# Low parts of split weights on another engine, and one unit further ahead

## The chip, the cores and the metric

The kernel runs on one core of one Trainium2 chip. The metric is the time of one launch in device microseconds, median of three runs. The engines' names in the rows are PE (TensorE matmuls), PEld (TensorE weight loads), DVE (VectorE), ACT (ScalarE), POOL (GpSimd) and SP (SyncE, which issues most loads).

## The reference

256 tokens of 1024 features pass through three blocks of float32 layers, one after the other:

```
x = first_block(x):    # two layers
    layer 0: mix = [ssd_mixer(x @ w_in), short_conv(x @ w_in)] @ w_out     # Mamba-2 with a gated convolution
    layer 1: mix = sliding_window_attention(x @ w_qkv) @ w_o               # 16 heads of 64, window 128
    both:    x = layer_norm(alpha * x + mix)
             x = layer_norm(alpha * x + (silu(x @ w_gate) * (x @ w_up)) @ w_down)
             x = x + (p @ w_ple) * sigmoid(x @ w_ple_gate + b)
x = second_block(x, c):
    h = rms_norm(x) * (1 + scale) + shift;  z = h @ w_in
    x = x + gate * ([rwkv7(z), stick_breaking_attention(z)] @ w_out)
    x = x + gate2 * moe(rms_norm(x) * ...)                                  # 32 experts, top 4, 403 MB
x = third_block(x, c):
    proj = (rms_norm(x) * (1 + scale) + shift) @ w_in                       # 14 column groups
    y_mla = attention(rms(q_lat) @ w_uq, rms(kv_lat) @ w_ukv);  y_mb = moba(q, k, v)
    y = (g_a * (y_mla @ w_o_mla) + g_b * (y_mb @ w_o_moba)) @ w_out
    x = x + gate * rms_norm(y)
```

## The kernel before, in words

Activations lie feature-major, [128, 8, 256]. The blocks run in sequence: the SSD layer, its feed-forward part with the gated embedding (ple), the attention layer, its feed-forward part, the mixer of the second block, its experts, and the third block. Outside the experts every dense product works with split weights. A float32 weight tile w becomes a high part hi, rounded to the F32R format by a copy on ScalarE (tile `wh`, L309), and a low part lo = w - hi (tile `wl`, L310). The activations are split in the same way, and a product is three matmuls, hi·xh, hi·xl and lo·xh (helper `mm`, L511).

Weights arrive in a ring of eight 1 MB tiles, loaded on SyncE's queue in the order of a plan that is written ahead (class `Stream`). A unit is 128 x 1024 weights: one `wh`, one `wl`, and 24 matmuls of TensorE. `unit(name, n)` (L333) gives the next unit to its user, and splits units ahead until n are split that have not been used up (`ahead`, L317). So each call puts a copy into ScalarE's queue and a subtraction into that of GpSimd or VectorE at that place of the program. The pool of split parts has three buffers of each part. A load is issued when the last unit of an older tile has been split.

The low part goes to GpSimd for each third unit (u % 3 == 0), else to `self.rest`. That is VectorE, but GpSimd in the attention layer from the first head to the end of w_o (L1021 to L1029), and in the whole third block (L2229). The engines take their instructions in the order of the program, which is written by hand (a manual schedule); no planner moves anything. What VectorE has besides low parts are evictions of sums from PSUM, splits of activations, norms (a square root is a chain of small operations, `rsqrt1` at L530 to L545 with tiles q1..., `rsqrt` at L515 to L525 with tiles r4...), and the row maxima of the attentions.

The attentions (`attention`, L1034) run a head or two at a time between units of a dense product ("ticks"): a head's scores, the row maximum (L1049), its scaling (L1052), the exponent on ScalarE, the division of the probabilities (L1083), transposes, and the product with the values. The latent norm of the third block (L2300 to L2309) is such a background chain too. `rows_norm` (L654) takes the last two units of a layer's last product and computes the layer norm behind them.

Of the kernel before, what the change touches and what calls it, by code (L numbers as in the profile page):

```python
# [22 lines left out]
F32 = mybir.dt.float32  # L23
# [227 lines left out]
class Stream:  # L251


    def __init__(self, kb, plan, ring=8):
        self.kb, self.ring = kb, ring
        self.plan = []
        self.units = []
        self.fence = []
        unit = 1024
        for e in plan:  # L260
            if e == "end":
                self.fence.append(len(self.units))
                continue
            i = len(self.plan)
            self.plan.append(e)
            name, r0, nk, c0, n, split = e
            h = nk if not split else max(1, unit // n)
            for k in range(0, nk, h):
                self.units.append((i, k, min(h, nk - k), k + h >= nk, split))
        self.raws = {}  # L270
        self.splits = {}
        self.nsplit = self.used = 0
        self.pending = None
        self.rest = kb.nc.vector
        self.room, self.nload = ring, 0

    def _retire(self, i):
        self.room += 1
        self.load()
# [19 lines left out]
    def _split(self, u):  # L299
        kb = self.kb  # L300
        i, k0, nk, last, split = self.units[u]
        if not split:
            return
        n = self.plan[i][4]
        self.load()
        w = self.raws[i][:, k0:k0 + nk, :]
        hi = kb.tl(kb.hpool, [128, nk, n], F32R, "wh")
        lo = kb.tl(kb.hpool, [128, nk, n], F32R, "wl")
        kb.nc.scalar.activation(hi, w, AF.Copy)  # L309
        (kb.nc.gpsimd if u % 3 == 0 else self.rest).tensor_sub(lo, w, hi.bitcast(F32))  # L310
        self.splits[u] = (hi, lo)
        if last:
            self._retire(i)
# [16 lines left out]
        self.ahead(n)  # L330
        return u

    def unit(self, name, n=2):  # L333

        return self.splits.pop(self._next(name, n))

    def raw(self, name, n=2):

# [47 lines left out]
class KB:  # L386
# [196 lines left out]
    def dense_F(self, name, x, nk=8, n=512, tag="acc", tail=False, ready=None, ticks=1):  # L583


        ps = [self.tl(self.pp, [128, 2, T], F32, tag) for _ in range((n + 255) // 256)]
        k = 0
        held = []
        while k < nk:
            if ready:  # L590
                ready(k)
            step = max(1, 1024 // n)
            last = k + step >= nk
            if tail and k + 2 * step >= nk and not last:
                held.append((k, self.st.unit(name)))
                k += step
                continue
            held.append((k, self.st.unit(name, 1 if held else 2)))
            for b in range(len(ps)):
                for k0, (hi, lo) in held:  # L600
                    for kk in range(hi.shape[1]):
                        for c in range(2 * b, min(2 * b + 2, (n + 127) // 128)):
                            s = slice(c * 128, min(n, c * 128 + 128))
                            self.mm3(ps[b][0:s.stop - s.start, c % 2], (hi[:, kk, s], lo[:, kk, s]),
                                     (x[0][:, k0 + kk], x[1][:, k0 + kk]), start=(k0 + kk == 0 and c % 2 == 0))
            k += step
            held = []
            for _ in range(ticks):
                self.tick()
        return ps  # L610
# [43 lines left out]
    def rows_norm(self, name, x, nk, ps, nm, i, fill, parts=None, ready=None):  # L654


        nc, P = self.nc, self.xpool
        self.rows_T(name, x, 0, nk - 2, ps, ready)
        if ready:
            ready(nk - 1)  # L660
        us = [(nk - 2, self.st.unit(name)), (nk - 1, self.st.unit(name, 1))]
        xn = self.tl(P, [128, 2, 1024], F32, "xn")
        half = [slice(0, 512), slice(512, 1024)]
        for t in range(2):
# [29 lines left out]
        xf = self.tl(self.fpool, [128, 8, T], F32, "xf")  # L694
# [273 lines left out]
    def att_layer(self, xf, x):  # L968
        nc = self.nc
# [5 lines left out]
        for u in range(4):  # L975
            hi, lo = self.st.unit("w_qkv")
            for kk in range(2):
                k = u * 2 + kk
# [35 lines left out]
        for h in range(2):  # L1014
            ps = self.dense_F("w_qkv", x, ticks=1 + h)
            for j in range(4):
                c = 4 * h + j
                nc.vector.tensor_scalar(qT[:, c], ps[j // 2][:, j % 2], self.col("b_qk", c), 0.125, op0=OP.add, op1=OP.mult)
            if h == 0:
                self.bg = self.attention(P, [head(i) for i in range(16)], self.band, 1.0)  # L1020
                self.st.rest = nc.gpsimd  # L1021
        ps = self.residual(xa, self.ident)

        def ready(k):
# [1 line left out]
                self.tick()  # L1026

        r = self.rows_norm("w_o", ox, 8, ps, "lnm", 1, self.cond_fill(1), ready=ready)
        self.st.rest = nc.vector  # L1029
        es.close()  # L1030
        return r

# [258 lines left out]
    def mixer(self, xf, stat):  # L1291
        nc, pp, st = self.nc, self.pp, self.st
        es = ExitStack()
        X = self.xpool
# [3 lines left out]
        vs = self.tl(P, [128, 2, 512], F32, "m")  # L1298
        hes = ExitStack()
        self.hpool = hes.enter_context(self.pool("wsplit2", 3))  # L1300
        self.st.fence.pop(0)
        t4 = lambda tag: self.tl(P, [128, 4, T], F32, tag)
        c4 = lambda ap: ap.rearrange("p j (t s) -> p j t s", s=128)
        S = math.exp(-0.5)
        x = (self.tl(X, [128, 8, T], F32R, "xh"), self.tl(X, [128, 8, T], F32R, "xl"))
# [169 lines left out]
        hes = ExitStack()  # L1475
# [15 lines left out]
        hes = ExitStack()  # L1491
# [731 lines left out]
    def third(self, xf, stat, P):  # L2223
        nc, pp = self.nc, self.pp
        es = ExitStack()
        X = self.xpool
        hes = ExitStack()
        self.hpool = hes.enter_context(self.pool("wsplit4", 3))
        self.st.rest = nc.gpsimd  # L2229
        t4 = lambda tag, dt=F32: self.tl(P, [128, 4, T], dt, tag)  # L2230
        x = (self.tl(X, [128, 8, T], F32R, "xh"), self.tl(X, [128, 8, T], F32R, "xl"))
        self.ada_norm(xf, X, self.col("g_pre", 0, 8), self.mod3[:, 8:16], self.mod3[:, 0:8], x, stat, 3, 8)
        dense = lambda **kw: self.dense_F("w_in_3", x, **kw)
        two = lambda ap: ap[:, 0:1].to_broadcast([128, 2, T])
        ag = self.tl(P, [128, 8], F32, "ag")
# [180 lines left out]
        for i in (1, 0):  # L2416
            g[i] = self.tl(X if i == 0 else P, [128, 8, T], F32, "xn" if i == 0 else "gb")
            for h in range(2):
                ps = dense()
                for j in range(4):  # L2420
                    k = 4 * h + j
                    nc.scalar.activation(g[i][:, k], ps[j // 2][:, j % 2], AF.Tanh, bias=hb[:, 8 * i + k:8 * i + k + 1], scale=0.5)

        for i, name in ((1, "moba"), (0, "mla")):
# [3 lines left out]
            if i == 0:  # L2428
                x = (self.tl(X, [128, 8, T], F32R, "xh"), self.tl(X, [128, 8, T], F32R, "xl"))
# [42 lines left out]
    def run(self):  # L2472
        nc, tc = self.nc, self.tc
        with ExitStack() as es:
# [4 lines left out]
            self.wpool = es.enter_context(self.pool("w", 8))  # L2479
            self.xpool = es.enter_context(self.pool("x", 1))  # L2480
            hes = ExitStack()
            self.hpool = hes.enter_context(self.pool("wsplit", 3))
            self.pp = outer.enter_context(tc.tile_pool(name="ps", bufs=2, space=PSUM))
            outer.enter_context(tc.manual_schedule())
            _tl = self.tl
# [8 lines left out]
            xf = self.tl(self.fpool, [128, 8, T], F32, "xf")  # L2494
# [11 lines left out]
            if "ssd" in self.stages:  # L2506
                xf, x, ready = self.ssd_layer(xf)
                xf, x = self.ffn_ple(0, xf, x, ready)
                self.dbg("xc0", xf)
            else:  # L2510
                stat = None
                x = self.resplit(xf, self.xpool)
            if "att" in self.stages:
                xf, x, ready = self.att_layer(xf, x)
                xf, stat = self.ffn_ple(1, xf, x, ready)
# [45 lines left out]
```

## Time and profile before

| | |
|---|---|
| median of three runs | 2303.5 us (2303.3 to 2306.31) |
| the profiled execution | 2300.47 us, its span 2298.7 us |
| mean granted clock of TensorE | 0.973 |
| TensorE busy | 2140.1 us (93%) |
| VectorE busy | 1038.7 us (45%) |
| ScalarE busy | 725.5 us (32%) |
| GpSimd busy | 452.9 us (20%) |
| DMA | 618.06 MB, of them 403 MB experts |

The layers run to 806 us, the mixer from there to 1080, the experts to 2026, the third block to the end. The rows below come from five views. Windows give for each stretch (start and end in us, then its length) the busy time of each engine in us with its instructions in brackets, then the granted clock of TensorE as a share of full speed, the share of the DMA engines that is busy, and GB/s. Waits give the engine, operation and line that waited, the releaser, and the us in total, the times and the longest. The view of a line gives the operation, count, shortest, median and longest in ns. The timeline gives start and duration in us, engine, line, operation, output and inputs. Groups of instructions give busy us and mean ns of one, then the idle time before them.

### The profile page before, as it was taken

The numbers are of one execution on the slowest core, as the hardware profiler recorded it, in microseconds if no ns is written. First come the engines' busy times: TensorE is split into PE (matmuls) and PEld (weight loads), VectorE is DVE, ScalarE is ACT, GpSimd is POOL, SyncE is SP. The second block draws the span as 40 slices with busy tenths as digits, with TensorE's granted clock in tenths as the row PEclk, the third lists the DMA queues.
The fourth block names the chain that finished last, engine by engine and source line by source line (L and its number), as shares of the span: only waits on it lengthen the run. The fifth ranks groups of instructions, "written<-read, shape, count | busy, mean of one in ns | idle before, by whom it ended". The sixth has DMA issues, their size and how long they took to land.

```text
span 2298.7 us, 31686 instructions
## 1 busy us (share of the span) xinstructions
PE 2140.1 (93%) x13242; PEld 1505.3 (65%) x13242; DVE 1038.7 (45%) x1937; ACT 725.5 (32%) x1169; POOL 452.9 (20%) x220
## 2 busy tenths in 40 slices
PE   7999999989999987888899999999999999989997
PEld 7897998887898877778444444344443333377886
DVE  6674676556677658756222222322222211144653
ACT  5444543545543553333111110111111011033552
POOL 2322232223232234221000000000000000056453
PEclk9999999999999999989899999999999999999998
DMA  7434767432767632105799999999999999963320
GB/s 297 157 130 146 274 262 272 177 129 74 282 261 284 233 127 83 65 1 204 317 426 427 427 423 427 427 428 427 428 428 427 428 427 427 426 242 132 114 70 19
DMA packets 62100, 618.06 MB, mean 269 GB/s; under 512 B 7648, under 2 KB 10720, under 8 KB 12672
## 3 DMA queue, kind: packets, MB, share of 16 engines
q1 hardware_dynamic: 58768, 612.33, 66.3%
q10 hardware_dynamic: 3184, 3.65, 0.5%
q8 instruction: 106, 1.74, 0.3%
q14 instruction: 42, 0.34, 0.0%
HBM read 614.90 MB, written 1.05 MB: 268 GB/s over the span
## 4 chain that ended last, share of the span: by engine, by line
PE 34%; DMA 12%; DVE 4%; ACT 1%; issue 0%; POOL 0%; ACTq 0%; DVEq 0%; SPq 0%; POOLq 0%
PE acc L511 21%; DMA expert<-exp_w 12%; PE py L511 10%; PE tp L511 2%; DVE an L1052 1%; PE tp L2036 0%; DVE pr L1083 0%; ACT pr L1075 0%; PE tp L2028 0%; DVE am L1049 0%; DVE q1t L543 0%; POOL wl L310 0%; DVE kf L2357 0%; DVE qf L2465 0%; DVE ot L2399 0%
## 5 line engine op out<-in xcount | busy, mean ns | idle before, releaser
L511 PE MATMUL acc<-xh,wh 128*128 128x256 f32 (+1 forms) x1736 | 496.0, 289 | 16.1 <-ACT wh L309 13.0
L511 PE MATMUL acc<-xh,wl 128*128 128x256 f32 (+2 forms) x1704 | 485.8, 285 | 18.3 <-POOL wl L310 9.4
L511 PE MATMUL acc<-xl,wh 128*128 128x256 f32 (+1 forms) x1736 | 487.9, 285 | 1.4 <-DVE xl L1284 1.3
L511 PE MATMUL acc<-expert,xe 128*64 128x512 f32 x2048 | 457.0, 597 | 18.0 <-DMA expert<-exp_w 15.7
L511 PEld LDWEIGHTS acc<-xh,wh 128*128 128x128 f32 (+1 forms) x1736 | 330.0, 191 | 24.7 <-ACT wh L309 13.6
L511 PEld LDWEIGHTS acc<-expert,xe 128*64 128x64 f32 x2048 | 144.8, 137 | 299.4 <-issue 282.0
L511 PEld LDWEIGHTS acc<-xh,wl 128*128 128x128 f32 (+2 forms) x1704 | 326.0, 191 | 22.6 <-POOL wl L310 11.5
L511 PEld LDWEIGHTS acc<-xl,wh 128*128 128x128 f32 (+1 forms) x1736 | 329.8, 191 | 4.8 <-DVE xl L1284 1.9
L310 POOL TENSOR_TENSOR wl<-w_w_in,wh 128x1024 fp32r<-128x1024 f32 (+1 forms) x49 | 119.0, 2435 | 1079.0 <-ACT wh L309 1068.5
L511 PE MATMUL py<-expert,aT 128*64 128x512 f32 x1024 | 235.3, 602 | 4.0 <-DMA expert<-exp_w 3.3
L2011 ACT ACTIVATE s<-a 128x512 f32<-128x512 f32 x32 | 20.2, 630 | 529.9 <-DVE a L2010 529.8
L2071 DVE SCALAR_TENSOR_TENSOR xf<-py,mod,xf 128x256 f32<-128x256 f32 x128 | 55.6, 479 | 279.8 <-PE py L511 279.8
L2010 DVE TENSOR_SCALAR a<-acc 128x512 f32<-128x512 f32 x32 | 22.1, 692 | 346.3 <-PE acc L511 346.3
L511 PEld LDWEIGHTS py<-expert,aT 128*64 128x64 f32 x1024 | 72.1, 138 | 138.2 <-issue 128.8
L1224 DVE SCALAR_TENSOR_TENSOR w_ada_t<-w_ada_t,pe 128x1024 f32<-128x1024 f32 x56 | 93.2, 1687 | 0.0
L309 ACT ACTIVATE wh<-w_w_in 128x1024 fp32r<-128x1024 f32 (+1 forms) x66 | 68.4, 1046 | 38.0 <-PE acc L511 32.0
L2058 ACT ACTIVATE y<-py 64x512 f32<-64x512 f32 x64 | 37.9, 592 | 117.5 <-PE py L511 116.9
L511 PE MATMUL tp<-sel,xh 128*128 128x128 f32 x512 | 63.5, 285 | 7.9 <-ACT aT L2038 6.9
L309 ACT ACTIVATE wh<-w_w_ffn_down 128x1024 fp32r<-128x1024 f32 x44 | 46.8, 1064 | 69.3 <-PE acc L511 69.3
L511 PE MATMUL acc<-wh,hh 128*128 128x512 f32 x176 | 68.7, 390 | 0.0
L511 PE MATMUL acc<-wh,hl 128*128 128x512 f32 x176 | 68.5, 389 | 0.0
L511 PE MATMUL acc<-wl,hh 128*128 128x512 f32 x176 | 68.5, 389 | 0.0
(659 smaller groups left out, 3405.0 us busy)
## 6 DMA issues: line engine op xcount, KB each, us to landing
expert<-exp_w SPq DMA_DIRECT2D x191, 2048.0 KB, 28.9
w_w_in<-tiles SPq DMA_DIRECT2D x31, 1024.0 KB, 4.8
w_ada_t<-tiles SPq DMA_DIRECT2D x28, 1024.0 KB, 6.9
w_w_ffn_gate<-tiles SPq DMA_DIRECT2D x22, 1024.0 KB, 4.8
w_w_ffn_up<-tiles SPq DMA_DIRECT2D x22, 1024.0 KB, 5.6
w_w_ffn_down<-tiles SPq DMA_DIRECT2D x22, 1024.0 KB, 5.6
w_w_in_mix<-tiles SPq DMA_DIRECT2D x21, 1024.0 KB, 7.4
w_w_out_mix<-tiles SPq DMA_DIRECT2D x8, 1024.0 KB, 4.8
```

The costliest lines, as they stand in the source:

```text
L309: kb.nc.scalar.activation(hi, w, AF.Copy)
L310: (kb.nc.gpsimd if u % 3 == 0 else self.rest).tensor_sub(lo, w, hi.bitcast(F32))
L511: self.nc.tensor.matmul(out, lhsT, rhs, start=start, stop=True, skip_group_check=True)
L1052: nc.vector.tensor_scalar(nm, m, -scale, None, op0=OP.mult)
L1224: self.nc.vector.scalar_tensor_tensor(w[:, j], w[:, j], 1.0, crow[:, int(m >= 48)], op0=OP.mult, op1=OP.mult, accum_out=dst)
L2010: nc.vector.tensor_scalar(a, pg, 7.0, None, op0=OP.min)
L2011: nc.scalar.activation(s, a, AF.Sigmoid, scale=1.702)
L2058: nc.scalar.activation(y[r, o], py[r], AF.Copy)
L2071: nc.vector.scalar_tensor_tensor(xf[:, k], ps[o][:, c], gate2(k), xf[:, k], op0=OP.mult, op1=OP.add)
```

## The change

Three things change. `Stream._split` picks the engine of a low part by a rule: GpSimd only for each third unit of `w_in_mix`, `w_out_mix`, `w_out_3`, of `w_in_3` but for one column group, and of the feed-forward weights but for their first piece; VectorE for all others, those of the attention layer's w_qkv and w_o, of the ple gates, of the mixer and of two thirds of the third block among them. `unit` splits three units ahead where it split two (`self.depth`), in the layers and in the third block; the mixer sets it back to two. The pools of split parts have four buffers of each part in the layers and in the third block. The stretches of raw weights keep their two.

```
@@ -271,8 +271,8 @@
         self.splits = {}
         self.nsplit = self.used = 0
         self.pending = None
-        self.rest = kb.nc.vector
         self.room, self.nload = ring, 0
+        self.depth = 3
 
     def _retire(self, i):
         self.room += 1
@@ -307,7 +307,10 @@
         hi = kb.tl(kb.hpool, [128, nk, n], F32R, "wh")
         lo = kb.tl(kb.hpool, [128, nk, n], F32R, "wl")
         kb.nc.scalar.activation(hi, w, AF.Copy)
-        (kb.nc.gpsimd if u % 3 == 0 else self.rest).tensor_sub(lo, w, hi.bitcast(F32))
+        name, r0, _, c0, _, _ = self.plan[i]
+
+        far = u % 3 == 0 and (name in ("w_in_mix", "w_out_mix", "w_out_3") or name == "w_in_3" and c0 != 928 or name[:5] == "w_ffn" and r0 + c0)
+        (kb.nc.gpsimd if far else kb.nc.vector).tensor_sub(lo, w, hi.bitcast(F32))
         self.splits[u] = (hi, lo)
         if last:
             self._retire(i)
@@ -330,9 +333,9 @@
         self.ahead(n)
         return u
 
-    def unit(self, name, n=2):
-
-        return self.splits.pop(self._next(name, n))
+    def unit(self, name, n=None):
+
+        return self.splits.pop(self._next(name, n or self.depth))
 
     def raw(self, name, n=2):
 
@@ -595,7 +598,7 @@
                 held.append((k, self.st.unit(name)))
                 k += step
                 continue
-            held.append((k, self.st.unit(name, 1 if held else 2)))
+            held.append((k, self.st.unit(name, self.st.depth - len(held))))
             for b in range(len(ps)):
                 for k0, (hi, lo) in held:
                     for kk in range(hi.shape[1]):
@@ -658,7 +661,7 @@
         self.rows_T(name, x, 0, nk - 2, ps, ready)
         if ready:
             ready(nk - 1)
-        us = [(nk - 2, self.st.unit(name)), (nk - 1, self.st.unit(name, 1))]
+        us = [(nk - 2, self.st.unit(name)), (nk - 1, self.st.unit(name, self.st.depth - 1))]
         xn = self.tl(P, [128, 2, 1024], F32, "xn")
         half = [slice(0, 512), slice(512, 1024)]
         for t in range(2):
@@ -1018,7 +1021,6 @@
                 nc.vector.tensor_scalar(qT[:, c], ps[j // 2][:, j % 2], self.col("b_qk", c), 0.125, op0=OP.add, op1=OP.mult)
             if h == 0:
                 self.bg = self.attention(P, [head(i) for i in range(16)], self.band, 1.0)
-                self.st.rest = nc.gpsimd
         ps = self.residual(xa, self.ident)
 
         def ready(k):
@@ -1026,7 +1028,6 @@
                 self.tick()
 
         r = self.rows_norm("w_o", ox, 8, ps, "lnm", 1, self.cond_fill(1), ready=ready)
-        self.st.rest = nc.vector
         es.close()
         return r
 
@@ -1298,6 +1299,7 @@
         vs = self.tl(P, [128, 2, 512], F32, "m")
         hes = ExitStack()
         self.hpool = hes.enter_context(self.pool("wsplit2", 3))
+        self.st.depth = 2
         self.st.fence.pop(0)
         t4 = lambda tag: self.tl(P, [128, 4, T], F32, tag)
         c4 = lambda ap: ap.rearrange("p j (t s) -> p j t s", s=128)
@@ -2225,11 +2227,10 @@
         es = ExitStack()
         X = self.xpool
         hes = ExitStack()
-        self.hpool = hes.enter_context(self.pool("wsplit4", 3))
-        self.st.rest = nc.gpsimd
+        self.hpool = hes.enter_context(self.pool("wsplit4", 4))
         t4 = lambda tag, dt=F32: self.tl(P, [128, 4, T], dt, tag)
         x = (self.tl(X, [128, 8, T], F32R, "xh"), self.tl(X, [128, 8, T], F32R, "xl"))
-        self.ada_norm(xf, X, self.col("g_pre", 0, 8), self.mod3[:, 8:16], self.mod3[:, 0:8], x, stat, 3, 8)
+        self.ada_norm(xf, X, self.col("g_pre", 0, 8), self.mod3[:, 8:16], self.mod3[:, 0:8], x, stat, 2, 8)
         dense = lambda **kw: self.dense_F("w_in_3", x, **kw)
         two = lambda ap: ap[:, 0:1].to_broadcast([128, 2, T])
         ag = self.tl(P, [128, 8], F32, "ag")
@@ -2479,7 +2480,7 @@
             self.wpool = es.enter_context(self.pool("w", 8))
             self.xpool = es.enter_context(self.pool("x", 1))
             hes = ExitStack()
-            self.hpool = hes.enter_context(self.pool("wsplit", 3))
+            self.hpool = hes.enter_context(self.pool("wsplit", 4))
             self.pp = outer.enter_context(tc.tile_pool(name="ps", bufs=2, space=PSUM))
             outer.enter_context(tc.manual_schedule())
             _tl = self.tl
```

Line numbers move by up to three: L310 is L313 in the new kernel, L545 is L548, L1049 is L1050. By the order of both kernels, 79 low parts leave GpSimd for VectorE; TensorE and SyncE have the same instructions in the same order.

The first place is the end of the SSD layer on VectorE: the last low parts in front of the layer norm (`bst` are its statistics). Before:

```order
L310 TENSOR_TENSOR wl_2144<-w_w_out_mix_1670,wh_2143 128x1024
L310 TENSOR_TENSOR wl_2178<-w_w_out_mix_1728,wh_2177 128x1024
L310 TENSOR_TENSOR wl_2196<-w_w_out_mix_1804,wh_2195 128x1024
L310 TENSOR_TENSOR wl_2230<-w_w_ffn_gate_36_2113,wh_2229 128x1024
L675 BN_STATS bst_2290<-acc_1894 128x6
L675 BN_STATS bst_2290<-acc_1895 128x6
L676 BN_AGGR bmv_2291<-bst_2290 128x2
L535 TENSOR_SCALAR q1v_269_2296<-bmv_2291 128x1
L538 TENSOR_SCALAR q1y_272_2299<-q1v_269_2296 128x1
```

After:

```order
L313 TENSOR_TENSOR wl_2132<-w_w_out_mix_1646,wh_2131 128x1024
L313 TENSOR_TENSOR wl_2166<-w_w_out_mix_1704,wh_2165 128x1024
L313 TENSOR_TENSOR wl_2184<-w_w_out_mix_1780,wh_2183 128x1024
L313 TENSOR_TENSOR wl_2218<-w_w_ffn_gate_36_2101,wh_2217 128x1024
L313 TENSOR_TENSOR wl_2234<-w_w_ffn_gate_36_2101,wh_2233 128x1024
L678 BN_STATS bst_2290<-acc_1898 128x6
L678 BN_STATS bst_2290<-acc_1899 128x6
L679 BN_AGGR bmv_2291<-bst_2290 128x2
L538 TENSOR_SCALAR q1v_269_2296<-bmv_2291 128x1
L541 TENSOR_SCALAR q1y_272_2299<-q1v_269_2296 128x1
```

One more low part of the first feed-forward piece stands in VectorE's queue ahead of the norm; before, the one that was split last there was GpSimd's.

The second place is the start of the third block, on VectorE: the first norm (q1v, q1y, q1h, q1t are its square root). Before:

```order
L2071 SCALAR_TENSOR_TENSOR xf_7643<-py_14413,mod_14_122,xf_7643 128x256 x2
L2071 SCALAR_TENSOR_TENSOR xf_7643<-py_14414,mod_14_122,xf_7643 128x256 x2
L1265 SCALAR_TENSOR_TENSOR ada_14475<-mod_15_123,cols_95 128x8
L537 TENSOR_SCALAR q1v_1852_14491<-tp_14425 128x2
L538 TENSOR_SCALAR q1y_1855_14494<-q1v_1852_14491 128x2
L539 TENSOR_SCALAR q1h_1853_14492<-q1v_1852_14491 128x2
```

and GpSimd, at the same place:

```order
L310 TENSOR_TENSOR wl_14478<-w_w_in_0_14454,wh_14477 128x1024
L310 TENSOR_TENSOR wl_14482<-w_w_in_0_14454,wh_14481 128x1024
L310 TENSOR_TENSOR wl_14488<-w_w_in_1_14456,wh_14487 128x1024
L310 TENSOR_TENSOR wl_14578<-w_w_in_1_14456,wh_14577 128x1024
L310 TENSOR_TENSOR wl_14608<-w_w_in_2_14458,wh_14607 128x1024
L310 TENSOR_TENSOR wl_14636<-w_w_in_2_14458,wh_14635 128x1024
```

After, VectorE:

```order
L1266 SCALAR_TENSOR_TENSOR ada_14475<-mod_15_123,cols_95 128x8
L313 TENSOR_TENSOR wl_14478<-w_w_in_0_14454,wh_14477 128x1024
L313 TENSOR_TENSOR wl_14482<-w_w_in_0_14454,wh_14481 128x1024
L540 TENSOR_SCALAR q1v_1850_14487<-tp_14425 128x2
L541 TENSOR_SCALAR q1y_1853_14490<-q1v_1850_14487 128x2
L542 TENSOR_SCALAR q1h_1851_14488<-q1v_1850_14487 128x2
L546 SCALAR_TENSOR_TENSOR q1t_1852_14489<-q1y_1853_14490,q1h_1851_14488 128x1 x2
L548 SCALAR_TENSOR_TENSOR q1y_1853_14490<-q1t_1852_14489,q1y_1853_14490 128x1 x2
```

and GpSimd's first rows of the block:

```order
L313 TENSOR_TENSOR wl_14642<-w_w_in_3_14460,wh_14641 128x1024
L2251 TENSOR_TENSOR qm_14550<-qm_14550,rope_120 128x512
L313 TENSOR_TENSOR wl_14739<-w_w_in_4_14462,wh_14738 128x832
L2251 TENSOR_TENSOR qm_14550<-qm_14550,rope_120 128x512
L2267 MEMSET kz_1886_14804 64x1024
```

Two low parts stand ahead of the norm on VectorE, where GpSimd had three beside it; GpSimd's first low part is now the one of the fourth column group.

The third place is the attention of the third block on VectorE, the first heads (am is a row maximum, an its scaling, pr the probabilities). Before:

```order
L2357 TENSOR_TENSOR kf_14943<-rt_15310 32x2048
L1049 TENSOR_REDUCE am_15348<-py_15344 128x1 x2
L1052 TENSOR_SCALAR an_15351<-am_15348 128x2
L1081 RECIPROCAL as_15354<-as_15354 128x2
L1083 TENSOR_SCALAR pr_15353<-pr_15353,as_15354 128x128
L1083 TENSOR_SCALAR pr_15353<-pr_15353,as_15354 128x256
L1049 TENSOR_REDUCE am_15394<-py_15390 128x1 x2
```

After:

```order
L1050 TENSOR_REDUCE am_15354<-py_15350 128x1 x2
L1053 TENSOR_SCALAR an_15357<-am_15354 128x2
L1082 RECIPROCAL as_15360<-as_15360 128x2
L1084 TENSOR_SCALAR pr_15359<-pr_15359,as_15360 128x128
L1084 TENSOR_SCALAR pr_15359<-pr_15359,as_15360 128x256
L313 TENSOR_TENSOR wl_15367<-w_w_in_15_14955,wh_15366 128x1024
L1050 TENSOR_REDUCE am_15398<-py_15394 128x1 x2
L1053 TENSOR_SCALAR an_15401<-am_15398 128x2
```

A low part stands between the probabilities of one head and the row maximum of the next. Beside these places, in the latent norm two low parts stand ahead of the chain on VectorE and one behind it, in front of the scaling of the latents (L2310); before, there were none.

## Rows read from the trace of the kernel before

**Rows 1.** Windows by stage: layers, mixer, experts, third block.

```profile
0.00:806.00 806.00, 762.66 (x5440) 699.40 (x5441) 513.08 (x826) 382.58 (x554) 223.04 (x108) 0.99 0.58 213
806.00:1080.00 274.00, 230.39 (x1677) 208.78 (x1677) 181.24 (x378) 108.86 (x174) 81.83 (x45) 0.93 0.23 82
1080.00:2026.00 946.00, 908.68 (x4441) 383.91 (x4441) 210.94 (x488) 121.58 (x230) 0.17 (x1) 0.98 0.99 418
2026.00:2299.00 273.00, 238.39 (x1690) 213.18 (x1688) 133.43 (x247) 112.51 (x212) 147.83 (x67) 0.93 0.30 105
```

**Rows 2.** Windows of five short stretches, columns as above.

```profile
60.00:80.00 20.00, 15.60 (x127) 15.00 (x127) 17.93 (x25) 7.25 (x9) 4.97 (x2) 1.00 0.38 135
234.00:246.00 12.00, 10.55 (x73) 9.90 (x74) 7.40 (x16) 6.75 (x12) 0.00 (x0) 0.86 1.00 404
1100.00:1110.00 10.00, 7.78 (x45) 6.08 (x46) 2.35 (x6) 2.79 (x5) 0.00 (x0) 0.83 0.03 10
2091.00:2096.00 5.00, 4.46 (x21) 4.46 (x22) 1.68 (x6) 0.00 (x0) 0.00 (x0) 0.50 0.63 210
2255.00:2268.00 13.00, 8.62 (x44) 8.01 (x44) 5.33 (x6) 4.10 (x5) 8.05 (x4) 0.74 0.00 1
```

**Rows 3.** The line of the low parts: ns shortest, median, longest.

```profile
L310 DVE TENSOR_TENSOR wl<-w_w_in_mix,wh x30: 1215/1220/3416, 13.6 to 165.4; 128x1024 fp32r<-128x1024 f32 x30
...
L310 POOL TENSOR_TENSOR wl<-w_w_o,wh x8: 2342/2370/2381, 511.6 to 565.7; 128x1024 fp32r<-128x1024 f32 x8
```

**Rows 4.** Waits of TensorE in the layers: us in total, times, longest.

```profile
PE acc L511 <- DVE wl L310: 6.8, 7, 1.7
PE acc L511 <- POOL wl L310: 5.7, 5, 1.9
```

**Rows 5.** Timeline of VectorE and GpSimd in the layers' two norms.

```profile
227.82 0.16 DVE L545 SCALAR_TENSOR_TENSOR q1y<-q1t,q1y 128x1 f32<-128x1 f32 x1
...
228.26 2.34 DVE L545 SCALAR_TENSOR_TENSOR q1y<-q1t,q1y 128x1 f32<-128x1 f32 x1
...
228.22 2.38 POOL L310 TENSOR_TENSOR wl<-w_w_ffn_gate,wh 128x1024 fp32r<-128x1024 f32 x1 [4.54 <-ACT wh L309]
...
573.60 2.38 DVE L545 SCALAR_TENSOR_TENSOR q1y<-q1t,q1y 128x1 f32<-128x1 f32 x1
```

**Rows 6.** Waits of TensorE in the mixer.

```profile
PE acc L511 <- POOL wl L310: 3.7, 2, 1.9
...
PE acc L511 <- DVE wl L310: 3.6, 4, 2.7
```

**Rows 7.** Timeline, third block: first norm, GpSimd beside it, and the last norm.

```profile
2030.84 4.48 DVE L543 SCALAR_TENSOR_TENSOR q1t<-q1y,q1h 128x1 f32<-128x1 f32 x2
...
2028.34 6.96 POOL L310 TENSOR_TENSOR wl<-w_w_in,wh 128x1024 fp32r<-128x1024 f32 x3 [948.17 <-ACT wh L309]
...
2286.80 0.35 DVE L543 SCALAR_TENSOR_TENSOR q1t<-q1y,q1h 128x1 f32<-128x1 f32 x2
```

**Rows 8.** Waits of TensorE in the third block.

```profile
PE tp L1258 <- DVE q1y L545: 7.1, 2, 5.3
PE tp L2306 <- DVE r4y L525: 4.5, 1, 4.5
PE acc L511 <- POOL wl L310: 3.9, 2, 1.9
```

**Rows 9.** Timeline of the latent norm, VectorE, then GpSimd.

```profile
2085.23 2.33 DVE L520 TENSOR_SCALAR r4t<-r4t 128x4 int32<-128x4 int32 x1
2087.59 0.16 DVE L523 TENSOR_TENSOR r4h<-r4t 128x4 f32<-128x4 f32 x1
...
2088.18 2.33 DVE L523 TENSOR_TENSOR r4h<-r4y 128x4 f32<-128x4 f32 x1
...
2088.15 2.34 POOL L310 TENSOR_TENSOR wl<-w_w_in,wh 128x1024 fp32r<-128x1024 f32 x1 [0.62 <-ACT wh L309]
```

**Rows 10.** Groups of VectorE in the third block: busy us, mean ns.

```profile
L1052 DVE TENSOR_SCALAR an<-am 128x2 f32<-128x2 f32 x16 | 18.1, 1130 | 0.5
```

More of the change, by code (lines that the diff above doesn't have):

```diff
@@ L273, in __init__ @@
         self.pending = None
-        self.rest = kb.nc.vector
         self.room, self.nload = ring, 0
+        self.depth = 3
     def _retire(self, i):
@@ L309, in _split @@
         kb.nc.scalar.activation(hi, w, AF.Copy)
-        (kb.nc.gpsimd if u % 3 == 0 else self.rest).tensor_sub(lo, w, hi.bitcast(F32))
+        name, r0, _, c0, _, _ = self.plan[i]
+        far = u % 3 == 0 and (name in ("w_in_mix", "w_out_mix", "w_out_3") or name == "w_in_3" and c0 != 928 or name[:5] == "w_ffn" and r0 + c0)
+        (kb.nc.gpsimd if far else kb.nc.vector).tensor_sub(lo, w, hi.bitcast(F32))
         self.splits[u] = (hi, lo)
@@ L331, in _next, with unit @@
         return u
-    def unit(self, name, n=2):
-        return self.splits.pop(self._next(name, n))
+    def unit(self, name, n=None):
+        return self.splits.pop(self._next(name, n or self.depth))
     def raw(self, name, n=2):
@@ L597, in dense_F @@
                 continue
-            held.append((k, self.st.unit(name, 1 if held else 2)))
+            held.append((k, self.st.unit(name, self.st.depth - len(held))))
             for b in range(len(ps)):
@@ L660, in rows_norm @@
             ready(nk - 1)
-        us = [(nk - 2, self.st.unit(name)), (nk - 1, self.st.unit(name, 1))]
+        us = [(nk - 2, self.st.unit(name)), (nk - 1, self.st.unit(name, self.st.depth - 1))]
         xn = self.tl(P, [128, 2, 1024], F32, "xn")
@@ L1020, in att_layer @@
                 self.bg = self.attention(P, [head(i) for i in range(16)], self.band, 1.0)
-                self.st.rest = nc.gpsimd
         ps = self.residual(xa, self.ident)
@@ L1028, in att_layer @@
         r = self.rows_norm("w_o", ox, 8, ps, "lnm", 1, self.cond_fill(1), ready=ready)
-        self.st.rest = nc.vector
         es.close()
@@ L1300, in mixer @@
         self.hpool = hes.enter_context(self.pool("wsplit2", 3))
+        self.st.depth = 2
         self.st.fence.pop(0)
@@ L2227, in third @@
         hes = ExitStack()
-        self.hpool = hes.enter_context(self.pool("wsplit4", 3))
-        self.st.rest = nc.gpsimd
+        self.hpool = hes.enter_context(self.pool("wsplit4", 4))
         t4 = lambda tag, dt=F32: self.tl(P, [128, 4, T], dt, tag)
         x = (self.tl(X, [128, 8, T], F32R, "xh"), self.tl(X, [128, 8, T], F32R, "xl"))
-        self.ada_norm(xf, X, self.col("g_pre", 0, 8), self.mod3[:, 8:16], self.mod3[:, 0:8], x, stat, 3, 8)
+        self.ada_norm(xf, X, self.col("g_pre", 0, 8), self.mod3[:, 8:16], self.mod3[:, 0:8], x, stat, 2, 8)
         dense = lambda **kw: self.dense_F("w_in_3", x, **kw)
@@ L2481, in run @@
             hes = ExitStack()
-            self.hpool = hes.enter_context(self.pool("wsplit", 3))
+            self.hpool = hes.enter_context(self.pool("wsplit", 4))
             self.pp = outer.enter_context(tc.tile_pool(name="ps", bufs=2, space=PSUM))
```

## The prediction

> **What bounds the kernel now.** I read the windows by stage first, then what TensorE waited for in each, then the timelines of the places where those waits stand. The windows [rows 1] show two kernels in one. In the 946 us of the expert stage DMA is busy 0.99 at 418 GB/s: the bytes of the weights set it, and the change touches nothing there. In the layers (806 us), the mixer (274) and the third block (273) TensorE is busy 762.66, 230.39 and 238.39 us, so it is idle 43.3 + 43.6 + 34.6 = 121.5 us, and no other engine is above 67%. There the matmuls are the bound, and only TensorE's idle time and its slow clock can be won or lost. That time is paid one for one: before the expert stage too, since at 1100 to 1110 the DMA share is 0.03 [rows 2], that is, the expert buffers are full and the loads wait for the first buffer to be used up. Whoever reaches that point earlier starts the DMA-bound stretch earlier.
>
> **The change part by part.** All sums are against the profiled execution, 2300.47 us (its span of 2298.7 and 1.8 around it); the median of three runs is 3.0 us above it.
>
> *Work moved.* TensorE's and SyncE's instructions keep their order. By the order of the two kernels 79 low parts go from GpSimd (151 before, 72 after) to VectorE (168 before, 247 after): 25 in the layers, 12 in the mixer, 42 in the third block. One costs 2.37 us on GpSimd and 1.22 on VectorE [rows 3]. VectorE gets 79 × 1.22 = 96.4 us more: 513 + 30 of 806, 181 + 15 of 274, 133 + 51 of 273. It stays under 72% in each, so the question is where the 1.22 us pieces stand in its queue.
>
> *Waits for split weights in the layers.* TensorE waits 6.8 us for low parts of VectorE and 5.7 for those of GpSimd [rows 4], 12.5 in all. Splitting three units ahead gives a unit one unit more of matmuls to be ready in; the longest single wait is 1.9 us, less than the 2.37 that a low part lasts. So most of it goes. At 60 to 80 us, where VectorE is busy 17.93 of 20 [rows 2], it is not lateness of issue but a full VectorE, and I leave 3 us there. Ends 0 and −12.5, taken −9.5.
>
> *The two norms of the layers.* Here GpSimd's low part starts at 228.22 and lasts 2.38; VectorE's one-element operation starts at 228.26 and lasts 2.34, against 0.16 for the same operation 0.4 us earlier; the second norm has it at 573.60 [rows 5]. Two operations that start together end together: VectorE stands still until GpSimd's is through. In the order after, this low part is on VectorE ahead of the norm's statistics, where it has the whole wait for the last matmuls to run in. Gain 2 × (2.34 − 0.16) = 4.4. Behind the first, the granted clock is 0.86 over 12 us [rows 2]: 1.7 us lost, 3.4 for the two if the second is like it. The norm's own idle time remains, so I count half, 1.7. Ends 0 and −7.8, taken −6.
>
> *The mixer.* GpSimd keeps none of its low parts; depth and buffers stay. Its waits are 3.7 for GpSimd's and 3.6 for VectorE's low parts [rows 6]. The first go where VectorE is free in time; the second may grow, since 12 × 1.22 = 14.6 us are queued among the work of two mixers. Ends +14.6 (all on the path) and −7.3, taken −4, nearer the rows of what is waited for now.
>
> *The start of the third block.* Three GpSimd low parts run from 2028.34 for 6.96 us, and a pair of one-element operations that takes 0.35 us at 2286.80 takes 4.48 [rows 7]; TensorE waits for the result of this chain, 5.3 us at the longest of two waits [rows 8]. The order after puts two low parts on VectorE ahead of the norm and none on GpSimd. Gain 4.1, against one low part (1.2) that I expect still to run when the norm's sum arrives; with two it is 2.4. If the collisions stay for another reason, that 2.4 is the loss. Ends +2.4 and −4.1, taken −2.9.
>
> *The latent norm.* TensorE waits 4.5 us for r4y [rows 8]. In that chain two operations take 2.33 us where their like takes 0.16, one under a GpSimd low part at 2088.15 [rows 9]: 2 × 2.17 = 4.3. The 5 us behind the wait run at a granted clock of 0.50 [rows 2], the lower of the two levels: 2.5 lost. After, two of three low parts stand ahead of or behind this chain on VectorE. Ends 0 and −7, taken −6.
>
> *The end of the third block.* TensorE waits 3.9 us for GpSimd's low parts in the block [rows 8], the longest in front of the last product, and the 13 us behind run at 0.74 [rows 2], 3.4 lost. After, two in three of these low parts take 1.22, and they are issued one unit earlier; the norm's idle time between merge and last product stays. Ends 0 and −7.3, taken −4.5.
>
> *What is late next.* Each low part on VectorE holds up what stands behind it: evictions, and in the attentions the row maxima of the next head. No row shows that price. From below: before, 168 low parts on VectorE brought 6.8 + 3.6 = 10.4 us of waits, 0.062 each, and 79 × 0.062 = 4.9. From above: all 79 on the path, 96.4 us, which would need a VectorE without idle time. Below nothing it can go too: the 16 scalings of the third block that follow the row maxima take 1.13 us each [rows 10], where operations of like size take 0.16 [rows 9], that is 15.5 us of standing still behind GpSimd, of which the chain of heads can win back a part. I take +5, since the waits that VectorE's low parts now cause are the nearest row.
>
> The Trainium skill (Perfetto Trace Analysis, section Optimizing Scalar/DVE Operations) speaks against the change: offload a full VectorE, to GpSimd at need, but as the two share a read port of SBUF, moving work between those two might not help. The trace agrees that they hinder each other (2.34 against 0.16), but in the window of the layers VectorE is at 64% and GpSimd at 28%, so neither is full. By that page's last words alone the gain would be about nothing.
>
> Sum: −9.5 − 6 − 4 − 2.9 − 6 − 4.5 + 5 = −27.9. Profiled, 2300.5 − 27.9 = 2272.6; as a median, 3.0 more: 2275.5.
>
> **The rivals.**
> - *Everything named goes.* All best ends: −12.5 − 7.8 − 7.3 − 4.1 − 7 − 7.3 = −46, and nothing new late: 2257.5. For it: the longest waits are short against a unit. Against it: the mixer keeps its depth, and a norm's own chain is not shortened to nothing.
> - *VectorE takes the place of the waits.* The collisions go (−4.4 − 4.1 + 1.2 − 4.3 = −11.6) and the waits for split weights only change their name. About 2292. For it: 17.93 of 20 us at 60 to 80. Against: VectorE's share of the stages.
> - *Nothing is gained.* Low parts cost VectorE in its queue what GpSimd cost it in collisions: 2303.5. A time within 0.2% (4.6 us) is what a measurement of this kernel cannot tell from no change.
> - *Slower: low parts in the attentions.* In the order after, 7 low parts of w_o and 14 of the third block stand between one head's scaling and the next head's row maximum. The head's matmuls wait for that chain. If each of the 21 ends on TensorE's path, that is 25.6 us, and 14.6 of the mixer with it, 40.2, against −28.9 of the other terms (the sum without the mixer and without what is late next): +11.3, 2314.8. It decides if a head's chain does not fit into the matmuls of one unit. Against it: GpSimd's collisions lengthen the same chain now [rows 10], and one low part on VectorE is half as long as one on GpSimd [rows 3].
>
> **How the numbers follow.** My forecast 0.60, everything 0.14, VectorE in its place 0.16, nothing 0.04, slower 0.06. The predicted time is 2275.5. The range of 8 in 10 goes from 2259 (just short of the full case) to 2293 (it takes in the case of VectorE in its place); outside lie part of the full case, nothing and slower. Faster by over 0.2% 0.90, within 0.2% 0.04, slower 0.06.
>
> **What would show it.** In the profile after: no VectorE operation of one element above 1 us in the two norms of the layers and at the start of the third block; the r4y wait under 1 us; the waits for low parts in the layers at 3 us or so; VectorE's busy time up by less than 96 us, since the collisions leave it; the clock behind the norms nearer 1. The expert stage keeps its 946 us, and starts some 17 us earlier (9.5 + 6 + 4, less 37/79 of the 5). I am wrong if VectorE's low parts lead the list of waits in the attentions, or if row maxima, evictions or xn show waits of TensorE that the rows of before don't have.

## The result, and the profile after

The changed kernel takes 2274.9 us (median of 4 runs, 2268.43 to 2278.14) against 2304.9 us before in the same comparison. The ratio is 0.9873 with a 95% interval of 0.9859 to 0.9887, that is 30 us less. The forecast was 2275.5. The profiled execution of the changed kernel is the fastest of its four, 2268.43 us; its span is 2266.6 us, 32.1 less than the one before.

The total came out as forecast, its parts did not. TensorE runs the same 13242 matmuls in the same order in both kernels, so the start of each can be set against the start of the same matmul before. At the end of a stage the difference tells how far TensorE is ahead by then:

| stage, in time of the kernel before | forecast | measured in this stage | ahead at its end |
|---|---|---|---|
| layers, to 806 us | -15.5 | -19.2 | -19.2 |
| mixer, to 1080 us | -4.0 | -10.4 | -29.6 |
| experts, to 2024 us | 0 | **+18.3** | -11.3 |
| third block, to 2288 us | -13.4 | -20.3 | -31.6 |
| "what is late next", anywhere | +5 | not found | |

The stages' windows of the changed kernel, cut at the same matmuls, answer to [rows 1] (start and end, length, busy us of PE, PEld, DVE, ACT, POOL, then granted clock, DMA share, GB/s):

```profile
0.00:786.90 786.90, 759.55 (x5441) 698.86 (x5442) 530.79 (x851) 382.00 (x554) 162.25 (x83) 0.99 0.59 219
786.90:1050.40 263.50, 231.35 (x1677) 209.94 (x1676) 178.13 (x390) 108.83 (x174) 51.85 (x33) 0.94 0.12 41
1050.40:2014.70 964.30, 913.25 (x4441) 385.69 (x4440) 210.36 (x487) 121.48 (x230) 0.00 (x0) 0.98 1.00 422
2014.70:2266.60 251.90, 229.86 (x1690) 205.77 (x1688) 149.87 (x289) 111.98 (x212) 47.94 (x25) 0.97 0.32 113
```

Three stages are shorter and the expert stage is longer: 964.3 us for the same matmuls that took 946. Its DMA share rose from 0.99 to 1.00. In the mixer it fell from 0.23 to 0.12, 82 to 41 GB/s: bytes that were loaded there before are now loaded in the expert stage. That the layers' VectorE is busy 530.79 us against 513.08, though 25 x 1.22 = 30 us were put on it, and in the whole kernel 1069.2 against 1038.7 with 96 us put on it, says that 66 us of what counted as busy before was time in which VectorE stood still. (In the third block 42 of 56 low parts moved, three quarters of them and not two thirds.)

TensorE's waits in the layers (12 to 810 us), the lines that answer to [rows 4]:

```profile
PE acc L514 <- DVE wl L313: 1.2, 2, 0.8
```

In the third block, answering to [rows 8] (r4y and the low parts of GpSimd have no line any more; one wait of 0.8 us for a low part of VectorE is new):

```profile
PE tp L1259 <- DVE q1y L548: 3.2, 2, 1.9
```

The timeline of the third block's first norm on VectorE, where [rows 7] had 4.48 us, the chain of the latent norm, where [rows 9] had 2.33 twice, and the scalings of the row maxima as a group (busy us, mean ns), which answers to [rows 10]:

```profile
2019.71 0.35 DVE L546 SCALAR_TENSOR_TENSOR q1t<-q1y,q1h 128x1 f32<-128x1 f32 x2
...
2069.17 0.17 DVE L523 TENSOR_SCALAR r4t<-r4t 128x4 int32<-128x4 int32 x1
...
2069.96 0.16 DVE L526 TENSOR_TENSOR r4h<-r4y 128x4 f32<-128x4 f32 x1
```

```profile
L1053 DVE TENSOR_SCALAR an<-am 128x2 f32<-128x2 f32 x16 | 5.7, 359 | 0.5
```

The operations of the two norms last what they last alone (0.35 us for the pair in [rows 7], 0.16 in [rows 9]), and the scalings are down from 1130 ns to 359 on average. The granted clock behind the layers' first norm, behind the latent norm and at the end, against 0.86, 0.50 and 0.74 in [rows 2]:

```profile
229.00:241.00 12.00, 11.02 (x89) 9.50 (x82) 9.06 (x19) 7.59 (x13) 0.00 (x0) 1.00 0.98 386
2071.00:2076.00 5.00, 5.00 (x40) 4.69 (x39) 3.56 (x6) 1.06 (x1) 0.00 (x0) 1.00 0.51 179
2224.00:2237.00 13.00, 9.68 (x80) 9.27 (x79) 10.07 (x13) 5.78 (x8) 2.21 (x1) 1.00 0.00 1
```

**Where the expert stage lost 18 us.** SyncE's timeline shows its loads (start, duration of the group, source, count). Before, then after:

```profile
916.68 138.29 SPq L373 DMA_DIRECT2D expert<-exp_w  x4
```

```profile
1052.79 4.16 SPq L376 DMA_DIRECT2D expert<-exp_w  x8
```

Before, the first load of expert weights was issued at 916.7 us, far inside the mixer; after, at 1052.8, at its very end. The waits of SyncE's queue between 870 and 1056 us in the changed kernel say for what:

```profile
SPq L376 <- DVE wl L313: 180.6, 1, 180.6
```

It stood for 180.6 us until a low part on VectorE was done. VectorE's timeline shows which one, the last of the mixer:

```profile
1051.54 1.22 DVE L313 TENSOR_TENSOR wl<-w_w_out,wh 128x1024 fp32r<-128x1024 f32 x1 [1.73 <-ACT wh L309]
```

The addresses in the two built programs explain it: a buffer can be loaded only when the last reader of what lay there before is done. The nine expert buffers, 16 KB of each partition each, lie over memory that the blocks before them used, four of them (e0 to e3) over the ring of weight tiles. Which of the mixer's last eight tiles (164 to 167 of w_in, 168 to 171 of w_out) lies where:

```
            before        after
  e0        165, 166      168, 171
  e1        164, 167      165, 169
  e2        169, 170      166, 167
  e3        168, 171      164, 170
```

The loads are issued in a fixed order, RING = [0, 1, 6, 7, 8, 2, 3, 5, 4] (L143), which suits the places before: e0 and e1 come free early, e3 last. After, e0 lies over tile 171, the last that is split, and eight loads stand behind it in SyncE's queue. No line of the diff names the ring or the experts. Just ahead of the first product of the experts, at 1100 to 1110 us of [rows 2], the DMA engines idled before, since the ring was full. At the same place of the program after, they are busy 0.99 of the time:

```profile
1071.50:1081.50 10.00, 5.63 (x31) 4.88 (x31) 1.39 (x5) 2.79 (x5) 0.00 (x0) 0.67 0.99 419
```

### The profile page after: what moved, and what is told of

Read it like the earlier page. It is cut to its first block, busy times and chain, and to the rows that moved or that the text cites. A ratio compares the mean times of both kernels' runs of the same rounds, so it can differ in the third digit from the quotient of the medians.

```text
span 2266.6 us, 31625 instructions
## 1 busy us (share of the span) xinstructions
PE 2134.0 (94%) x13242; PEld 1500.3 (66%) x13242; DVE 1069.2 (47%) x2016; ACT 724.3 (32%) x1169; POOL 262.0 (12%) x141
## 5 line engine op out<-in xcount | busy, mean ns | idle before, releaser
L313 POOL TENSOR_TENSOR wl<-w_w_in,wh 128x1024 fp32r<-128x1024 f32 (+1 forms) x11 | 26.7, 2428 | 1069.5 <-ACT wh L309 1049.6
L313 DVE TENSOR_TENSOR wl<-w_w_in,wh 128x1024 fp32r<-128x1024 f32 (+1 forms) x55 | 68.2, 1248 | 38.7 <-ACT wh L309 38.5
```

The source lines that it names most:

```text
L313: (kb.nc.gpsimd if far else kb.nc.vector).tensor_sub(lo, w, hi.bitcast(F32))
```

## The experiments

Each time is a median, with runs of the kernel before beside it: 2305.0 us for e1 to e4 and 2303.8 for e5 to e7 (2304.9 for the changed kernel). The stages are from one profiled execution each, by the start of the same matmuls, against the profiled execution of before:

| kernel | median | ratio, 95% interval | layers | mixer | experts | third | first expert load |
|---|---|---|---|---|---|---|---|
| changed kernel | 2274.9 | 0.9873 (0.9859 to 0.9887) | -19.2 | -10.4 | +18.3 | -20.3 | 1052.8 |
| e1_ring | 2255.9 | 0.9788 (0.9771 to 0.9804) | -22.0 | -5.1 | +0.7 | -18.1 | 902.1 |
| e2_engines | 2286.9 | 0.9921 (0.9904 to 0.9937) | +5.2 | -10.3 | +1.0 | -10.6 | 918.2 |
| e3_depth | 2306.7 | 1.0010 (1.0000 to 1.0021) | -10.8 | -1.5 | +18.5 | +0.1 | 1070.1 |
| e4_third_old | 2292.1 | 0.9939 (0.9922 to 0.9955) | -17.6 | -5.0 | +18.9 | +0.3 | 1059.8 |
| e5_ring_before | 2322.0 | 1.0081 (1.0059 to 1.0104) | +6.0 | -2.8 | +18.3 | +0.5 | 1085.6 |
| e6_heads_pool | 2262.5 | 0.9819 (0.9802 to 0.9836) | -16.0 | -6.3 | -0.8 | -15.1 | 908.2 |
| e7_all_vector | 2252.8 | 0.9773 (0.9747 to 0.9799) | -26.0 | -8.3 | +0.6 | -15.1 | 898.2 |

One caution for this table: e5 has the layers and the mixer of the kernel before, unchanged, and its execution is 6.0 us slower in the layers and 2.8 faster in the mixer than the one it is compared with. So a stage of one execution is known to some 6 us there, while the third block repeats within 1 us (unchanged in e4 and e5: +0.3 and +0.5).

**e1_ring: the order of the expert buffers.**

```
-RING = [0, 1, 6, 7, 8, 2, 3, 5, 4]
+RING = [2, 6, 7, 8, 1, 3, 0, 5, 4]
```

> The changed kernel, with the expert buffers taken in the order 2, 6, 7, 8, 1, 3, 0, 5, 4 instead of 0, 1, 6, 7, 8, 2, 3, 5, 4. Theory: splitting a unit further ahead gave the last weight tiles of the mixer other places in the ring of weight tiles; the first expert buffer now lies over the very last of them, so the first expert load waits until 1052.8 us (before: 916.7), and the expert stage gives back 18 of the 29.6 us that the layers and the mixer had won. With the new order the first load is issued near 890 to 910 us, TensorE stays 27 to 30 us ahead of the kernel before at the end of the experts (now 11.7), and the time is about 2258 (2253 to 2263). Rival: the experts' end is set by bytes and rate from a start that no order of buffers moves; the time stays at 2275 within 4.

Measured 2255.9 us, first load at 902.1:

```profile
902.07 154.05 SPq L376 DMA_DIRECT2D expert<-exp_w  x8
```

TensorE is 27.1 us ahead at the start of the experts and 26.4 at their end. One line gives back the lost 18 us (19 by the medians). The rival is out.

**e5_ring_before: the same fault put into the kernel before.**

```
-RING = [0, 1, 6, 7, 8, 2, 3, 5, 4]
+RING = [3, 1, 6, 7, 8, 2, 0, 5, 4]
```

> The kernel before with one change: expert buffer 3, which lies over the mixer's last weight tile, is taken first (order 3, 1, 6, 7, 8, 2, 0, 5, 4). Theory: the first expert load then waits for the last low part of the mixer (about 1080 us; 916.7 before), and the experts end at first load plus 954 us, as in the three kernels measured with a late first load (1052.8, 1059.8 and 1070.1 us with the experts' end at -11.3, -3.7 and +6.1 against before): here +16 to +19 us, 2321 to 2324 in all. Rival: what starts the experts is the first take of a buffer at 1111 us and the ring is full by then in any order: 2305 within 4.

Measured 2322.0, 18.3 us slower, first load at 1085.6 after a wait of 187.8 us for a low part, the experts' end at +21.5. The rule "first load plus a constant" gives +6.1 + (1085.6 - 1070.1) = +21.6. So the loss needs nothing of the change: a first buffer over the last tile is enough. In the four kernels with a late first load, the time from it to the end of the experts is the same within 0.6 us. There the stage ends with its loads, and what TensorE wins ahead of it counts only as far as it brings the last low part, and with it the first load, forward.

**e2_engines: the engine alone.**

```
-        (kb.nc.gpsimd if u % 3 == 0 else self.rest).tensor_sub(lo, w, hi.bitcast(F32))
+        name, r0, _, c0, _, _ = self.plan[i]
+        far = u % 3 == 0 and (name in ("w_in_mix", "w_out_mix", "w_out_3") or name == "w_in_3" and c0 != 928 or name[:5] == "w_ffn" and r0 + c0)
+        (kb.nc.gpsimd if far else kb.nc.vector).tensor_sub(lo, w, hi.bitcast(F32))
```

> The kernel before with the rule for the engine alone: two units ahead, three buffers. The tiles lie over the expert buffers as they do before. Theory: the engine ends the collisions (norms, third block) and the waits of the mixer, depth ends the waits for low parts in the layers; so here layers about -8, mixer -10, experts 0 (the gain passes), third block -14: about 2273 (2267 to 2280). Rival one, the depth does the work and the engine only the mixer's 10: about 2293. Rival two, more low parts on VectorE without the deeper split are late and cost time: above 2305.

Measured 2286.9, between the theory and rival one: the mixer has all of its gain, the third block half, and the layers none (+5.2, where unchanged code shows +6.0 in e5). TensorE's waits for low parts in the layers are 11.6 us, against 12.5 before:

```profile
PE acc L513 <- DVE wl L312: 7.5, 8, 1.7
PE acc L513 <- POOL wl L312: 4.1, 5, 1.0
```

The stretch of the ple gate (458 to 476 us) wins 3.7 us, and the two norms lose 2.2 and 2.9. VectorE at the first norm, with no collision left:

```profile
231.15 1.23 DVE L312 TENSOR_TENSOR wl<-w_w_ffn_gate,wh 128x1024 fp32r<-128x1024 f32 x1 [2.97 <-ACT wh L309]
232.29 1.29 DVE L677 BATCH_NORM_STATS2 bst<-acc 128x6 f32<-128x512 f32 x2
```

The low part now stands in front of the norm's statistics, and it waits 2.97 us for its high part; ScalarE's copy, at 230.05, had itself waited 1.61 us for matmuls to be done with a buffer. The statistics, ready or not, wait behind it: they start 7.2 us later than before, where TensorE is 3.0 us behind. These 4.2 us of delay outweigh the 2.2 that the collision cost. In the changed kernel, with a fourth buffer and the split one unit earlier, the same low part runs earlier, and the statistics start at 222.79, 2.3 us before those of the kernel before:

```profile
221.65 1.22 DVE L313 TENSOR_TENSOR wl<-w_w_ffn_gate,wh 128x1024 fp32r<-128x1024 f32 x1 [1.52 <-ACT wh L309]
```

**e3_depth: the depth alone** (three ahead and four buffers; the mixer stays at two; the diff is shown in part).

```
+        self.depth = 3
...
-            held.append((k, self.st.unit(name, 1 if held else 2)))
+            held.append((k, self.st.unit(name, self.st.depth - len(held))))
...
-            self.hpool = hes.enter_context(self.pool("wsplit", 3))
+            self.hpool = hes.enter_context(self.pool("wsplit", 4))
```

> The kernel before with the depth alone: three units ahead and four buffers in the layers and the third block, engines as before. Theory: layers about -12, mixer 0, third block about -4, but the first expert load waits for the last low part of the mixer, which is here near 1067 us, and the experts end 0 to 5 us later than before: in all about 2303 (2297 to 2309). Rival, the expert stage passes what is won ahead of it: about 2289.

Measured 2306.7, as the theory had it: TensorE is 12.3 us ahead at the end of the mixer, and 6.1 behind at the end of the experts. The addresses show that it is the depth that moves the tiles here: e3 has the places of the changed kernel, e2 those of before.

What the layers win, by the places that can be told apart, is the depth's. With the old engines the waits for low parts there fall to 0.4 us, the window of [rows 2] at 60 to 80 us is filled, and no operation of this line of the square roots takes longer than 163 ns:

```profile
PE acc L512 <- DVE wl L311: 0.4, 1, 0.4
60.00:80.00 20.00, 19.62 (x167) 19.41 (x166) 19.09 (x25) 8.03 (x9) 5.16 (x2) 1.00 0.45 158
L546 DVE SCALAR_TENSOR_TENSOR q1y<-q1t,q1y x60: 146/159/163, 182.8 to 2294.4; 128x1 f32<-128x1 f32 x60
```

GpSimd's low part at the first norm is still there, but it ends at 225.67 us, before the square root begins at 225.90. TensorE gains 3.5 and 1.6 us at the two norms and 5.9 at the ple gate, as much as in the changed kernel (3.4, 1.5, 5.9). The 7 to 11 us between e3's layers and those of the changed kernel, e1 and e4 are near the 6 us that unchanged code shows; what the engine adds there is open. So is which half of the depth does it, the unit further ahead or the fourth buffer: no run has them apart.

In the third block the depth alone does nothing (+0.1): GpSimd still makes all low parts there, and the scalings have the median of before, 1396 ns. The two halves of the change need each other there: -10.6 and +0.1 alone, -18 to -20 together.

**e4_third_old: the third block as before.**

```
-        self.hpool = hes.enter_context(self.pool("wsplit4", 4))
+        self.hpool = hes.enter_context(self.pool("wsplit4", 3))
+        self.st.depth = 2
+        self.st.old = True
...
-        (kb.nc.gpsimd if far else kb.nc.vector).tensor_sub(lo, w, hi.bitcast(F32))
+        (kb.nc.gpsimd if far or self.old else kb.nc.vector).tensor_sub(lo, w, hi.bitcast(F32))
```

> The changed kernel with the third block as before (all its low parts on GpSimd, two ahead, three buffers). Theory: everything up to the end of the experts as in the changed kernel, 11 to 12 us ahead of before, and the third block gives its 20 us back: 2293 to 2295. Rival: part of the third block's gain comes from the earlier part (a warmer clock, loads that are further), then 2285 to 2290.

Measured 2292.1, just under the theory's range and above the rival's, 17 us more than the changed kernel. The third block is at +0.3 us against before, which decides for the theory: its gain is its own. The "11 to 12 us ahead" at its start was 3.7 in this execution, whose first load is at 1059.8, 7 us later than in the changed kernel's, and whose experts end 7.6 us later. The place of the last low part in time passes to the end of the experts one for one.

**e6_heads_pool: low parts between the heads on GpSimd again** (on top of e1).

```
+        heads = name in ("w_o", "w_o_moba") or name == "w_in_3" and i >= 15
-        (kb.nc.gpsimd if far else kb.nc.vector).tensor_sub(lo, w, hi.bitcast(F32))
+        (kb.nc.gpsimd if far or heads else kb.nc.vector).tensor_sub(lo, w, hi.bitcast(F32))
```

> The changed kernel with the new order of expert buffers, and with the low parts that are made between the heads of the two attentions (w_o, w_o_moba, the last seven tiles of w_in_3) on GpSimd again. Theory: on VectorE these low parts cost no time that TensorE sees, and on GpSimd they stretch the scalings of the row maxima again: layers +0 to +2, third block +3 to +8, about 2261 (2257 to 2266). Rival, the low parts on VectorE hold up the heads' row maxima: GpSimd saves up to 25 us there, 2235 to 2252.

Measured 2262.5, in the range of the theory and 6.6 us over e1. The third block gives 3.0 back; the layers give 6.0, where the theory had 0 to 2, but that is no more than unchanged code shows. The scalings of the row maxima in the third block are again as long as in [rows 10]:

```profile
L1054 DVE TENSOR_SCALAR an<-am 128x2 f32<-128x2 f32 x16 | 18.1, 1130 | 0.5
```

The slower rival of the prediction is out with it: low parts in VectorE's queue cost the heads less than low parts beside it.

**e7_all_vector: no low part on GpSimd** (on top of e1; the tiles lie in other places again here, so it has a buffer order of its own, [3, 6, 7, 8, 1, 2, 0, 5, 4]).

```
-        (kb.nc.gpsimd if far else kb.nc.vector).tensor_sub(lo, w, hi.bitcast(F32))
+        kb.nc.vector.tensor_sub(lo, w, hi.bitcast(F32))
```

> The changed kernel with every low part on VectorE, and expert buffers in the order in which they come free here (3, 6, 7, 8, 1, 2, 0, 5, 4). Theory: the third on GpSimd is wanted where VectorE is near full, above all at 60 to 80 us of the layers, where it is busy 19 of 20 us already: layers +5 to +12, third block -2 to +2, about 2263 (2257 to 2270). Rival, GpSimd's low parts cost more in collisions than they save: 2243 to 2252.

Measured 2252.8: the theory is wrong, and the time is 0.8 us above the rival's range. VectorE gets 72 x 1.22 = 88 us more than in the changed kernel, and its busy time goes up by 9.4 (1078.6 against 1069.2). At 60 to 80 us, where I had read a full VectorE, it is less busy with more work, and TensorE has no idle time at all; answering to [rows 2]:

```profile
60.00:80.00 20.00, 20.00 (x172) 20.00 (x171) 17.50 (x28) 11.06 (x14) 0.00 (x0) 1.00 0.56 207
```

The changed kernel has 19.02 us of VectorE and 19.59 of TensorE in the same window, the kernel before 17.93 and 15.60. The layers are 4 us better than in e1 and the third block 3 worse; by the medians the two kernels stand 0.15% apart with intervals that overlap, so which is the better one, and with it the rival, is open. Both beat the changed kernel and the one before.

## Why the prediction was right, and where only by luck

- *Waits for split weights in the layers* (-9.5): right in kind and close in size. 12.5 us of waits became 1.2, and by e3 (0.4 left) and e2 (11.6 left) the deeper split does it. The 3 us left for the stretch at 60 to 80 us were a misreading: "not lateness of issue but a full VectorE". The depth alone wins 4.6 us there with VectorE busy 19.09 of 20, and e7 shows that part of this busy time was standing still beside GpSimd.
- *The two norms of the layers* (-6): the gain from before the norm to behind it is 3.4 us at the first (227 to 240 us) and 1.5 at the second (573 to 600). The size is near, but the step that named the engine as the cause failed. The move alone (e2) ends the collisions and loses 2.2 and 2.9 us, since the moved low part stands in front of the statistics and waits for its buffer; the depth alone (e3) has the whole gain with the low part still on GpSimd. I had said that on VectorE it would have "the whole wait for the last matmuls to run in"; that holds only with the deeper split and the fourth buffer.
- *Left out*: the ple gate at 458 to 476 us, 5.9 us, where TensorE waited 1.9 us for GpSimd's low part and ran at 0.92 of its clock. It is in the waits of [rows 4], but not its clock. The depth alone wins the same 5.9, the engine alone 3.7.
- *The mixer* (-4): -10.4 in the profiled execution, -5.0 to -5.1 in e1 and e4, which have the same mixer, and -1.5 and -2.8 in e3 and e5, whose mixer is unchanged. The sign holds in every run of the changed mixer, the size is known only to some 5 us.
- *The expert stage* (0): the step that failed. "Whoever reaches that point earlier starts the DMA-bound stretch earlier" was read from the row of before, where the ring is full at 1100 us, and silently took for granted that the loads would start as early as before. They started 136 us later, the stage gave back 18.3 us, and e1 and e5 show it from both sides. What would have told it in advance is in the built program, not in the trace: the first load's wait for the last tile. The order of instructions alone does not show it, as SyncE's is the same in both.
- *The third block* (-13.4): -20.3, and -18.1 in e1. Its start (2029 to 2036 us) gave 3.9 for 2.9, the latent norm with the slow clock behind it (2084 to 2100) 7.0 for 6, the end (2250 to 2270) 4.3 for 4.5, or 2.0 in e1. The rest, 4.9 us between 2100 and 2250, is the attentions, for which I had a price and no gain. With their low parts back on GpSimd (e6) 1.6 of it is left.
- *What is late next* (+5): wrong in sign. All waits of TensorE for low parts were 23.7 us before and are 5.4 after, and in the attentions of the third block it gained. The scalings there stood still for 15.5 us before; that this is what the heads win back is likely from e6, but not all of it: in e7, where none stands still, the same stretch wins 1.9 us, less than in the changed kernel.

Of the signs that the prediction named, those of the norms, of r4y, of the waits, of the busy time and of the clock came true. The one on the expert stage did not: it started 29.6 us earlier where 17 were named, and it did not keep its 946 us.

So it was luck that the sum of -27.9 was right to 4 us: three stages were too small by some 17 us, the +5 was not there, and one term that was taken as 0 is +18. Of the rivals, "everything named goes" (2257.5) is near the kernel without the fault of the ring: e1 has 2255.9. I had read the page of the Trainium skill that I weighed (Perfetto Trace Analysis, section Optimizing Scalar/DVE Operations: between VectorE and GpSimd moving work might not help as they share a read port) as no gain; e2, with the moved work alone, is 18 us faster. The trace agrees that GpSimd's work holds VectorE's up (2.34 us for an operation of 0.16, [rows 5]); here that speaks for the move onto one engine.

## What to carry to other kernels

Buffers of a later stage that lie over those of an earlier one inherit their last readers: after a change to any pool, depth or engine ahead, look again at what the first load of the next stage waits for, and put the buffers in the order in which they come free. If a DMA-bound stage follows, time won ahead of it passes through in full only as long as its loads start early enough for its buffers to be full at the first take; later than that, its end follows its first load. A change of two parts needs a run of each part alone: the engine looked like the cause at the layers' norms, and the depth was. VectorE's busy time includes standing still beside GpSimd, so a window that looks full may be emptied by giving it more of GpSimd's work (19.02 to 17.50 us of 20 here).

## What was not expected of the hardware

Where a small operation of VectorE falls on a subtraction of GpSimd, the two do not share the time; the small one can last as long as what is left of the large one (in [rows 5] both end at 230.60 us). The 16 scalings of 128x2 elements in the third block took 1.130 us on average with all of the block's low parts on GpSimd, 0.359 with a quarter of them left there, and 0.169 with none (e7):

```profile
L1053 DVE TENSOR_SCALAR an<-am 128x2 f32<-128x2 f32 x16 | 2.7, 169 | 0.5
```

That GpSimd's low parts, which take twice as long there, cost VectorE nearly as much as doing the work itself (88 us of subtractions added for 9.4 us of busy time) was more than I had reckoned with. The Trainium skill (SBUF — State Buffer, section Who interferes with whom) calls the ports that the two share an exclusive lock, and these rows agree.
